# Token-major products with reordered passes, batched norms, earlier operands and masks first in a two-layer decoder kernel

## The chip, the core and the metric

The kernel runs on one core of one Trainium2 chip. The metric is the device time of one execution in microseconds (us). Three runs of the kernel before took 1764.95, 1764.04 and 1764.25 us; the median is 1764.25.

## The reference

The program is a decoder trunk of two layers over 512 tokens of 1024 channels, all in float32. Cut to what matters here, each layer computes

```python
x = x + 0.5 * swiglu(rms_norm(x, ffn1_norm[l]), ffn1_w_in[l], ffn1_w_out[l])   # 1024 -> 2*2816 -> 1024
h = rms_norm(x, mix_norm[l]) @ w_mix_in[l]
(c_x, c_b, c_c, h_q, h_f, h_i, h_g, f_q, f_k, f_v, f_f) = jnp.split(h, split_at, axis=-1)
y = jnp.concatenate([short_conv_mixer(c_x, c_b, c_c, conv_w[l]),               # 256 columns
                     hgrn2_mixer(h_q, h_f, h_i, h_g, lower_bounds[l], ...),    # 4 heads of 64
                     fox_mixer(f_q, f_k, f_v, f_f, ...)], axis=-1)             # 8 heads of 64
x = x + y @ w_mix_out[l]
x = x + 0.5 * swiglu(rms_norm(x, ffn2_norm[l]), ffn2_w_in[l], ffn2_w_out[l])

# fox_mixer, one head, one block of 128 query tokens:
qh = rms_norm(q, q_gain) * 64 ** -0.5;  kh = rms_norm(k, k_gain);  cum = cumsum(log_sigmoid(f + f_bias))
s = qh @ kh.T + (cum[t] - cum[s]);  s = where(t >= s, s, -1e30);  o = softmax(s) @ v
```

## The kernel before

**Precision.** TensorE multiplies in the reduced format `fp32r`. Each float32 operand is therefore split into a high half (a cast on ScalarE, L435) and a low half (the rest, a subtraction on VectorE, L438), and every product is made of three passes into one PSUM bank: high by high (L451), the second pass with a low half (L457), and the third with the other low half (L458). Where the weights move through TensorE and the tokens are stationary, L457 is the pass with the weights' low half `lo`; where the tokens move, L457 and L458 are the two others in the same way. The split weights of two or three rows of tiles are one `hl` tile; there are three such buffers, and two `st` buffers for the loaded weights.

**Stages.** Layer 0's first feed-forward runs from 0 to 341 us of the span, its mixer's projections with HGRN2 to 462, its attention with the output product to 563. Then come the second feed-forward of layer 0 and the first of layer 1, to 1212, layer 1's projections to 1332, its attention to 1432, and its second feed-forward. The change touches the mixer stages of both layers.

**Projections.** Four products are "token-major" (`tokens`): four banks, three named `mm` and one `po`, hold the 128 x 512 results of the four blocks of 128 tokens, and the weights of 512 columns move through. One step of `stream_steps` (a granule) takes two rows of weight tiles: 2 rows x 4 banks x 3 passes = 24 matmuls, handed out in two halves of 12. HGRN2's small matmuls (L1494, 64 of them in a score group, whose bank VectorE empties with the masked copies of L1514) stand between the halves. `fox_qkv` makes two such products for the queries and keys of heads 0-3 and 4-7, and one for the values. ScalarE copies a finished bank into a `qk` tile (L1661). A list `later` holds the root-mean-square norms of the four blocks of a `qk` tile; one entry is issued per half granule (L1644-1655: square, sum, eight small operations on 128 x 8 numbers, and the scaling of 512 columns).

**Attention.** For each head, `prep` transposes a `qk` tile (four transposes, L1697), makes high and low halves (`b`, L1700 on ScalarE, L1701 on VectorE) and copies them with six transfers on the SP queue (L1708) into the stacked operands of the score matmuls. There are 16 steps (h, p), two for each head. `scores` (L1735) fills the score banks: for p = 0 one bank of 128 and 256 columns, for p = 1 two banks of 384 and 512. Each gets two fp32r matmuls and the causal mask, a bf16 matmul of the identity `identb` with `maskb`. VectorE takes the maximum (L1749), ScalarE the exponential and the scaling (L1755, L1757). `turn` transposes the weights `P` two steps later (L1772) and splits them into `PH` and `PL` (L1777, L1778); `values` (L1790) multiplies them with `V` into the `po` bank. At the end of a head, L1803 copies the lower half of the bank, L1804 adds it to the upper one in `fo`; after every second head `fyh` (L1807) and `fyl` (L1808) are the two halves of the 128 rows that go into the output product.

**Output product.** Beside the attention steps runs `most`: for each pair of 128 output channels, two banks take six rows of the mixer's outputs (convolution, HGRN2 and the first heads), three rows at a time, `w_mix_out` stationary and the outputs moving. The last two rows follow behind attention, with `late` passes (L535).

**What sets the order.** One generator per stage hands out dense work; the tables `HGRN_BESIDE` and `BESIDE` say how many half granules stand between two small steps. Where `follow` is called, the instructions of an engine are chained in the order in which they are written ("p" TensorE, "v" VectorE, "a" ScalarE, "s" SyncE); a scheduler places the others.

The loop that sets the order of an attention step is this one:

```python
for k, (h, p) in enumerate(steps):
    turn(h, p)
    if k + 2 < len(steps):
        scores(*steps[k + 2])
    if k:
        values(*steps[k - 1])
    if p == 0 and h + 2 < NH:
        prep(h + 2)
    yield
```

## Time and profile before

| what | us |
|---|---|
| median of three runs | 1764.25 |
| the profiled execution itself | 1765.45 |
| its span | 1763.3 |
| layer 0: projections and HGRN2 (341 to 462) | 121 |
| layer 0: attention and output product (462 to 563) | 101 |
| layer 1: the same two (1212 to 1332, 1332 to 1432) | 120, 100 |
| all else, the feed-forwards | 1321 |

The profile shows one execution. The rows speak of engines: PE is TensorE's matmuls, PEld its loads of stationary operands, DVE VectorE, ACT ScalarE, POOL GpSimd, SP SyncE. A row of the timeline gives the start in us, the duration, the engine, the line of the kernel, the operation and the tiles (out<-in), and in brackets an idle time before it with the instruction that ended it. Matmuls are pipelined: the duration of one is longer than the distance from its start to the next one's, so a loss is read from the starts.

### The profile page before, as it was taken

What the parts mean: (1) busy time and instruction counts of PE and PEld (TensorE: products, weight loads), DVE (VectorE), ACT (ScalarE), POOL (GpSimd) and SP (SyncE); (2) the same over time, 40 slices, a digit from 0 to 9 for tenths busy, and PEclk for the clock granted to TensorE, in tenths of its full rate; (3) what the DMA queues carried; (4) which work ended last, traced back from release to release, by engine and by line L of the source; (5) the groups of instructions that cost most, each with busy time, mean ns of one, the idle gap of its engine ahead of it and who ended that gap; (6) DMA issues with size and microseconds to landing.
All of it is one profiled execution on the core that took longest, in us unless ns stands there. A gap on an engine that the chain in (4) does not pass through costs nothing.

```text
span 1763.3 us, 33430 instructions
## 1 busy us (share of the span) xinstructions
PE 1753.8 (99%) x13613; PEld 1643.2 (93%) x13613; DVE 1416.0 (80%) x1956; ACT 1015.8 (58%) x1433; POOL 177.0 (10%) x174
## 2 busy tenths in 40 slices
PE   9999999999999999999999999999999999999999
PEld 7999999888888899999989999998888889999998
DVE  7988788679777898888679787876888779888783
ACT  5465555466666565555446656555657655655652
POOL 0011120100000111112001111201000001120200
PEclk9999999999999999999999999999999999999999
DMA  7768784243543776869267787923435438687762
GB/s 202 188 140 199 180 177 111 73 124 82 132 118 99 216 163 161 202 169 178 81 183 170 178 182 176 192 79 79 120 93 134 123 103 220 156 176 195 162 138 96
DMA packets 257465, 262.34 MB, mean 149 GB/s; under 512 B 25832, under 2 KB 236528, under 8 KB 257312
## 3 DMA queue, kind: packets, MB, share of 16 engines
q1 hardware_dynamic: 201456, 192.02, 36.4%
q0 software_dynamic: 55840, 68.19, 24.0%
q8 instruction: 107, 1.75, 0.4%
q14 instruction: 46, 0.38, 0.1%
q10 hardware_dynamic: 16, 0.00, 0.0%
HBM read 226.15 MB, written 2.17 MB: 129 GB/s over the span
## 4 chain that ended last, share of the span: by engine, by line
PE 90%; DVE 6%; ACT 2%; issue 1%; DMA 1%; SPq 0%; ACTq 0%; DVEq 0%
PE mm L451 12%; PE mm L458 12%; PE mm L457 12%; PE sc L458 6%; PE sc L451 6%; PE sc L457 6%; PE pt L457 6%; PE pt L451 6%; PE pt L458 6%; PE po L451 3%; PE po L458 3%; PE po L457 3%; DVE hl L438 1%; PE sc L1735 1%; PE po L1790 1%; PE pt L1772 1%
## 5 line engine op out<-in xcount | busy, mean ns | idle before, releaser
L916 DVE TENSOR_TENSOR hl<-w,hl 128x1024 fp32r<-128x1024 f32 x279 | 341.0, 1223 | 91.0 <-ACT hl L914 89.5
L914 ACT CAST hl<-w 128x1024 fp32r<-128x1024 f32 x279 | 292.6, 1049 | 198.3 <-PE mm L458 56.0
L438 DVE TENSOR_TENSOR hl<-st,hl 128x1024 fp32r<-128x1024 f32 (+3 forms) x152 | 160.4, 1056 | 103.0 <-ACT hl L435 101.4
L435 ACT CAST hl<-st 128x1024 fp32r<-128x1024 f32 (+3 forms) x151 | 137.4, 910 | 160.9 <-PE po L458 61.7
L451 PE MATMUL mm<-xc,hl 128*128 128x256 f32 x698 | 191.6, 275 | 0.6 <-ACT u L1034 0.6
L458 PE MATMUL mm<-xc,hl 128*128 128x256 f32 x696 | 191.6, 275 | 0.0
L457 PE MATMUL mm<-xc,hl 128*128 128x256 f32 x696 | 191.5, 275 | 0.0
L451 PE MATMUL pt<-xc,hl 128*128 128x256 f32 x546 | 149.7, 275 | 0.0
L457 PE MATMUL pt<-xc,hl 128*128 128x256 f32 x544 | 149.7, 275 | 0.0
L458 PE MATMUL pt<-xc,hl 128*128 128x256 f32 x544 | 149.6, 275 | 0.0
L451 PEld LDWEIGHTS mm<-xc,hl 128*128 128x128 f32 x698 | 133.9, 192 | 0.9 <-ACT u L1034 0.8
L458 PEld LDWEIGHTS mm<-xc,hl 128*128 128x128 f32 x696 | 133.6, 192 | 0.4 <-DVE hl L916 0.4
L457 PEld LDWEIGHTS mm<-xc,hl 128*128 128x128 f32 x696 | 133.6, 192 | 0.0
L458 PE MATMUL sc<-xc,hl 128*128 128x256 f32 x464 | 127.8, 275 | 0.1
L451 PE MATMUL sc<-xc,hl 128*128 128x256 f32 (+1 forms) x466 | 127.8, 275 | 0.0
L457 PE MATMUL sc<-xc,hl 128*128 128x256 f32 x464 | 127.7, 275 | 0.0
L451 PE MATMUL mm<-x,hl 128*128 128x512 f32 x272 | 105.9, 390 | 0.0
L451 PEld LDWEIGHTS pt<-xc,hl 128*128 128x128 f32 x546 | 104.7, 192 | 0.0
L457 PEld LDWEIGHTS pt<-xc,hl 128*128 128x128 f32 x544 | 104.4, 192 | 0.0
L458 PEld LDWEIGHTS pt<-xc,hl 128*128 128x128 f32 x544 | 104.4, 192 | 0.0
L457 PE MATMUL mm<-x,hl 128*128 128x512 f32 x272 | 103.1, 379 | 0.0
L458 PE MATMUL mm<-x,hl 128*128 128x512 f32 x272 | 103.1, 379 | 0.0
(520 smaller groups left out, 5595.9 us busy)
## 6 DMA issues: line engine op xcount, KB each, us to landing
w<-in_ffn_w_in_dram SPq DMA_DIRECT2D x124, 512.0 KB, 6.0
w<-in_ffn_w_out_dram POOLq DMA_DIRECT2D x50, 512.0 KB, 9.6
w<-in_ffn_w_out_dram SPq DMA_DIRECT2D x49, 512.0 KB, 4.5
st<-in_ffn_w_out_dram SPq DMA_DIRECT2D x39, 512.0 KB, 3.8
st<-in_w_mix_in_dram SPq DMA_DIRECT2D x72, 256.0 KB, 3.0
st<-in_ffn_w_in_dram SPq DMA_DIRECT2D x70, 256.0 KB, 3.5
w<-in_ffn_w_in_dram POOLq DMA_DIRECT2D x29, 512.0 KB, 10.1
w<-S POOLq DMA_DIRECT2D x29, 512.0 KB, 5.1
```

The source lines that it names most:

```text
L435: a = nc.scalar.copy(hi, src[:, c : c + w])
L438: b = nc.vector.tensor_sub(lo, src[:, c : c + w], hi)
L451: i = nc.tensor.matmul(acc[:, c], ah, bh[:, c.start // 2 : c.stop // 2, :], start=first and c.start == 0, stop=False, skip_group_check=True,)
L457: nc.tensor.matmul(acc, ah, bl, start=False, stop=False, skip_group_check=True)
L458: i = nc.tensor.matmul(acc, al, bh, start=False, stop=last, skip_group_check=True)
L914: A(nc.scalar.copy(hi, src))
L916: return lambda: V(nc.vector.tensor_sub(lo, src, hi))
L1735: mm = lambda *a, **k: E(nc.tensor.matmul(*a, skip_group_check=True, **k))
L1772: E(nc.tensor.transpose(tb[:, k * P : (k + 1) * P], to[u][:, j * P : (j + 1) * P], self.ident))
L1790: E(nc.tensor.matmul(self.ob[:, o], half[2][:, j, h].rearrange("p a d -> p (a d)"), part[:, at[0] : at[-1] + 1, :].rearrange("p b t -> p ( ...
```

## The change

The pieces are these.

1. `stream_steps` gets an argument `lows`. In the token-major products (`lows="held"`) the matmuls of each half granule are issued as all high-by-high and tokens-low passes first, and then all passes with the weights' low half. In the output product (`lows="moved"`) the first granule row keeps the three passes together; in the rows after it all passes with the high half of the outputs come first, and those with the low half last. Number and size of the matmuls stay.
2. The norms of the four blocks of a `qk` tile share their small operations: squares and sums go block by block, and then one operation on 128 x 32 numbers stands for four on 128 x 8. The list `later` gets six entries in place of four. VectorE's instructions fall by 58 in all, and ScalarE's by 36.
3. In a score group the mask is the first matmul of its bank, with `start=True`; the two masks of a p = 1 group stand side by side.
4. `prep(h + 2)` stands between `turn` and `scores`, where it stood behind `values`.
5. For the last head VectorE writes the lower rows of the high half `yh` straight from the bank; ScalarE casts only the first 64 rows, which are there earlier.

```diff
--- before.py
+++ after.py
@@ -465,7 +465,7 @@
     def stream_steps(
         self, jobs, parts_of, act, nk, mid=None, pre=None, deal=None, keep=False, lead=False,
-        fine=False, deep=2, rowwise=False, late=False,
+        fine=False, deep=2, rowwise=False, late=False, lows=None,
     ):
@@ -517,6 +517,30 @@
                 if end and not rowwise or lead and k == 0
                 else [(job, j) for j in range(kk) for job in jobs]
             )
+            if lows is not None:
+                if lows == "held":
+                    spans = [order[: len(order) // 2], order[len(order) // 2 :]]
+                    todo = [(x, i) for o in spans for ii in ((0, 2), (1,)) for x in o for i in ii]
+                else:
+                    n0 = len(jobs)
+                    todo = [(x, i) for x in order[:n0] for i in range(3)]
+                    todo += [(x, i) for ii in ((0, 2), (1,)) for x in order[n0:] for i in ii]
+                seen = set()
+                for n, (((acc, cols, toks, *more), j), i) in enumerate(todo):
+                    if n == len(todo) // 2:
+                        yield
+                    x = act(k + j)[i == (1 if lows == "moved" else 2)]
+                    w = rows[j][i == (2 if lows == "moved" else 1)][:, cols]
+                    last = end and all(y is not acc for (y, *_), _ in (t[0] for t in todo[n + 1 :]))
+                    self.follow("p", self.nc.tensor.matmul(
+                        acc, *((w, woven(x)) if toks is None else (x[:, toks], woven(w))),
+                        start=k == 0 and id(acc) not in seen, stop=last, skip_group_check=True,
+                    ))
+                    seen.add(id(acc))
+                k += kk
+                yield
+                continue
             for n, ((acc, cols, toks, *more), j) in enumerate(order):
                 if pre is not None and n == len(order) // 2:
                     pre(k, True)
@@ -1178,7 +1202,7 @@
                 bs = [self.bank(t) for t in ("mm", "mm", "mm", "po")]
                 yield from self.stream_steps(
                     [(bk, slice(0, T), t) for bk, t in zip(bs, TOK)], cols(*spans),
-                    self.xact, KD, lead=True, fine=True, **kw
+                    self.xact, KD, lead=True, fine=True, lows="held", **kw
                 )
                 return bs
@@ -1291,7 +1315,7 @@
                         for n, _ in enumerate(self.stream_steps(
                             [(bk, c, None) for bk, c in zip(banks, FM2)],
                             rows(0, 256 * dg, 256), act(0), 6, keep=True, fine=True, deep=3,
-                            rowwise=True,
+                            rowwise=True, lows="moved",
                         )):
                             if dg == 0 and n == 1:
                                 self.conv_out(ap_, 1, last)
@@ -1635,24 +1659,35 @@
                     later.pop(0)()
                 yield
-        def norm(qk, i):
-            x = qk[:, i].rearrange("p h w d -> p (h w) d")
-            sq = hp.tile([P, 8, HD], F32, tag="fs", name=self.n("fs"))
-            s8 = lambda tag: mp.tile([P, 8], F32, tag=tag, name=self.n(tag), bufs=2)
-            m, r, t = s8("fm"), s8("fr"), s8("ft")
-            nc.scalar.activation(sq, x, AF.Square)
-            nc.vector.reduce_sum(m, sq, axis=AX.X)
-            nc.vector.tensor_scalar(
-                m, m, scalar1=self.inv2[:, i : i + 1], scalar2=None, op0=ALU.mult
-            )
-            self.act(r, m, AF.Ln, bias=self.epsc)
-            self.act(r, r, AF.Exp, scale=-0.5)
-            self.rsqrt(r, m, r, t)
-            nc.vector.tensor_scalar(
-                r, r, scalar1=self.invc[:, i : i + 1], scalar2=None, op0=ALU.mult
-            )
-            nc.vector.tensor_mul(x, x, r.unsqueeze(2).to_broadcast([P, 8, HD]))
+        def norms(qk):
+            small = lambda tag: mp.tile([P, 4, 8], F32, tag=tag, name=self.n(tag), bufs=2)
+            m, r, t = small("fm"), small("fr"), small("ft")
+            wide = lambda a: a.unsqueeze(2).to_broadcast([P, 4, 8])
+            def squares(i):
+                x = qk[:, i].rearrange("p h w d -> p (h w) d")
+                sq = hp.tile([P, 8, HD], F32, tag="fs", name=self.n("fs"))
+                nc.scalar.activation(sq, x, AF.Square)
+                nc.vector.reduce_sum(m[:, i], sq, axis=AX.X)
+            def finish():
+                nc.vector.tensor_mul(m, m, wide(self.inv2))
+                self.act(r, m, AF.Ln, bias=self.epsc)
+                self.act(r, r, AF.Exp, scale=-0.5)
+                self.rsqrt(r, m, r, t)
+                nc.vector.tensor_mul(r, r, wide(self.invc))
+            def scale(i):
+                x = qk[:, i].rearrange("p h w d -> p (h w) d")
+                nc.vector.tensor_mul(x, x, r[:, i].unsqueeze(2).to_broadcast([P, 8, HD]))
+            later.append(lambda: squares(0))
+            later.append(lambda: squares(1))
+            later.append(lambda: squares(2))
+            later.append(lambda: (squares(3), finish()))
+            later.append(lambda: (scale(0), scale(1)))
+            later.append(lambda: (scale(2), scale(3)))
         for hf in range(2):
             qk = mp.tile([P, 4, 4, 2, HD], F32, tag="qk", name=self.n("qk"), bufs=2)
@@ -1662,7 +1697,7 @@
                     qk[:, i].rearrange("p h w d -> p w h d"),
                     bank.rearrange("p (h d w) -> p w h d", w=2, h=4),
                 )
-                later.append(lambda qk=qk, i=i: norm(qk, i))
+            norms(qk)
             half.append(qk)
         V = mp.tile([P, 4, NH, 2, HD], F32R, tag="V", name=self.n("V"))
         half.append(V)
@@ -1729,20 +1764,19 @@
                 at = [b[:, :P], b[:, P : 3 * P]]
             else:
                 at = [self.bank("sc")[:, : 3 * P], self.bank("sc")]
+            mm = lambda *a, **k: E(nc.tensor.matmul(*a, skip_group_check=True, **k))
+            if p == 0:
+                masked = [b.rearrange("p (b t) -> p b t", t=P)[:, ::2, :]]
+            else:
+                masked = [at[u][:, (2 + u) * P : (3 + u) * P] for u in range(2)]
+            for m in masked:
+                mask = self.maskb.unsqueeze(1).to_broadcast([P, 2, P]) if p == 0 else self.maskb
+                mm(m, self.identb, mask, start=True, stop=False)
             for u in range(2):
                 i = 2 * p + u
                 c, n = slice(i * P, (i + 1) * P), (i + 1) * P
-                mm = lambda *a, **k: E(nc.tensor.matmul(*a, skip_group_check=True, **k))
-                mm(at[u], QA[:, c], KA[:, :n], start=p == 1 or u == 0, stop=False)
-                mm(at[u], QB[:, c], KB[:, :n], start=False, stop=False)
-                if p == 1:
-                    mm(at[u][:, c], self.identb, self.maskb, start=False, stop=True)
-                elif u == 1:
-                    mm(
-                        b.rearrange("p (b t) -> p b t", t=P)[:, ::2, :], self.identb,
-                        self.maskb.unsqueeze(1).to_broadcast([P, 2, P]), start=False, stop=True,
-                    )
+                mm(at[u], QA[:, c], KA[:, :n], start=False, stop=False)
+                mm(at[u], QB[:, c], KB[:, :n], start=False, stop=True)
             to = [pb[:, :P], pb[:, P:]] if p == 0 else [pb[:, : 3 * P], pb[:, 3 * P :]]
             for u in range(2):
                 o = slice(u, u + 1)
@@ -1801,10 +1835,16 @@
             fo = self.fo
             ft = tl(self.tt, self.tb)
             nc.scalar.copy(ft[r, :], self.ob[64:, :])
+            if h == NH - 1:
+                kt = 4 + h // 2
+                nc.scalar.copy(self.yh[kt][:64, :], fo[:64, :])
+                nc.vector.tensor_add(self.yh[kt][r, :], self.ob[:64, :], ft[r, :])
             nc.vector.tensor_add(fo[r, :], self.ob[:64, :], ft[r, :])
             if h % 2:
                 kt = 4 + h // 2
-                nc.scalar.copy(self.yh[kt], fo)
+                if h < NH - 1:
+                    nc.scalar.copy(self.yh[kt], fo)
                 nc.vector.tensor_sub(self.yl[kt], fo, self.yh[kt])
         steps = [(h, p) for h in range(NH) for p in range(2)]
@@ -1817,12 +1857,12 @@
         yield
         for k, (h, p) in enumerate(steps):
             turn(h, p)
+            if p == 0 and h + 2 < NH:
+                prep(h + 2)
             if k + 2 < len(steps):
                 scores(*steps[k + 2])
             if k:
                 values(*steps[k - 1])
-            if p == 0 and h + 2 < NH:
-                prep(h + 2)
             yield
         values(*steps[-1])
```

TensorE in layer 0's attention, at a step in which `prep` stands. The tiles are `pt` for the transposes' banks, `sc` for the score bank, S and q for the operands of the scores. Before:

```order
L1772 MATMUL pt_5326<-ident,P_5197 128x128 x3
L1735 MATMUL sc_5335<-S_655_5216,S_654_5215 128x128
L1735 MATMUL sc_5335<-q_657_5218,q_656_5217 128x128
L1735 MATMUL sc_5335<-S_655_5216,S_654_5215 128x256
L1735 MATMUL sc_5335<-q_657_5218,q_656_5217 128x256
L1735 LDWEIGHTS identb
L1735 MATMUL sc_5335<-maskb,identb 128x2x128
L1697 MATMUL pt_5355<-ident,qk_4158 128x128 x4
```

TensorE at the same place in the changed kernel:

```order
L1806 MATMUL pt_5260<-ident,P_5131 128x128 x3
L1732 MATMUL pt_5273<-ident,qk_4158 128x128 x4
L1767 LDWEIGHTS identb
L1767 MATMUL sc_5289<-maskb,identb 128x2x128
L1767 MATMUL sc_5289<-S_637_5150,S_636_5149 128x128
L1767 MATMUL sc_5289<-q_639_5152,q_638_5151 128x128
L1767 MATMUL sc_5289<-S_637_5150,S_636_5149 128x256
L1767 MATMUL sc_5289<-q_639_5152,q_638_5151 128x256
```

The four transposes of `prep` and the mask moved from behind the score matmuls to the place ahead of them.

TensorE in the output product, the end of the second granule of the first pair of output channels, just ahead of the transposes of `P` (`cyh` is the high half of a convolution output, `fyh` and `fyl` are halves of the first heads' output). Before:

```order
L458 MATMUL mm_5848<-cyh_3684,hl_5941 128x512
L451 MATMUL mm_5847<-fyh_636_5142,hl_5941 128x512
L457 MATMUL mm_5847<-fyl_640_5146,hl_5941 128x512
L458 MATMUL mm_5847<-fyh_636_5142,hl_5941 128x512
L1772 MATMUL pt_5955<-ident,P_5818 128x128 x4
```

TensorE there in the changed kernel:

```order
L536 MATMUL mm_5782<-cyh_3684,hl_5875 128x512
L536 MATMUL mm_5781<-fyh_618_5072,hl_5875 128x512 x2
L536 MATMUL mm_5782<-fyh_618_5072,hl_5875 128x512
L1806 MATMUL pt_5889<-ident,P_5752 128x128 x4
L1806 MATMUL pt_5896<-ident,P_5752 128x128 x3
```

The pass with `fyl` left this half granule for the end of the next one, and a pass with `fyh` took its place.

VectorE in layer 0's projections, around the masked copies that empty HGRN2's score banks (`fr` is the norm's factor, `qk` the tile that it scales). Before:

```order
L438 TENSOR_TENSOR hl_4855<-st_4853,hl_4855 128x1024
L1652 TENSOR_SCALAR fr_4634<-fr_4634,invc_3901 128x8
L1514 COPY_PREDICATED A_4325<-lmask,sc_4647 128x64x2
L1655 TENSOR_TENSOR qk_4158<-qk_4158,fr_4634 128x512
L1514 COPY_PREDICATED A_4325<-lmask,sc_4648 128x64x2
L1471 TENSOR_TENSOR t_4685<-t_4689,q_3707 128x256
L1514 COPY_PREDICATED A_4325<-lmask,sc_4647 128x32x4
L1514 COPY_PREDICATED A_4325<-lmask,sc_4648 128x32x4
```

VectorE there in the changed kernel:

```order
L1683 TENSOR_TENSOR qk_4158<-qk_4158,fr_4474 128x512 x3
L438 TENSOR_TENSOR hl_4825<-st_4823,hl_4825 128x1024
L1538 COPY_PREDICATED A_4325<-lmask,sc_4610 128x64x2
L1538 COPY_PREDICATED A_4325<-lmask,sc_4611 128x64x2
L1538 COPY_PREDICATED A_4325<-lmask,sc_4610 128x32x4
L1538 COPY_PREDICATED A_4325<-lmask,sc_4611 128x32x4
```

The scalings of `qk` stand ahead of the weights' low half, and the four masked copies stand together behind it.

## The prediction

> **What bounds the kernel now.** I read the page first, then the busy time by stage, then the rows of TensorE in order of time wherever the distance from one matmul's start to the next is longer than the matmul's columns explain, and last the rows of the engine that each such gap names. Three lines of the page and two of the stages, layer 0's projections with HGRN2 and layer 0's attention with the output product (columns: stretch and its length; busy time of PE, PEld, DVE, ACT, POOL; granted clock; DMA share; GB/s):
>
> ```profile
> span 1763.3 us, 33430 instructions
> PE 1753.8 (99%) x13613; PEld 1643.2 (93%) x13613; DVE 1416.0 (80%) x1956; ACT 1015.8 (58%) x1433; POOL 177.0 (10%) x174
> PE 90%; DVE 6%; ACT 2%; issue 1%; DMA 1%; SPq 0%; ACTq 0%; DVEq 0%
> 341.00:462.00 121.00, 120.18 (x1113) 102.35 (x1113) 95.90 (x225) 74.87 (x147) 6.17 (x11) 1.00 0.43 108
> 462.00:563.00 101.00, 99.62 (x578) 86.13 (x577) 73.62 (x141) 65.44 (x141) 3.10 (x6) 1.00 0.44 117
> ```
>
> TensorE is busy 99% and carries 90% of the chain, at a granted clock of 1.00. No matmul of 512 or 256 columns is removed or added, so the time can fall only by gaps between matmuls, and rise only by new ones. The change touches the two mixer stages alone. So the work is to price each gap there, and to ask what each moved instruction will now keep waiting.
>
> **Token products: the pass with the weights' low half goes last.** The first granule of the first token product in layer 0:
>
> ```profile
> 376.23 0.38 PE L451 MATMUL mm<-hl,x 128*128 128x512 f32 x1
> 377.20 0.48 PE L457 MATMUL mm<-hl,x 128*128 128x512 f32 x1 [0.59 <-DVE hl L438]
> 377.52 0.38 PE L458 MATMUL mm<-hl,x 128*128 128x512 f32 x1
> 375.93 1.22 DVE L438 TENSOR_TENSOR hl<-st,hl 128x1024 fp32r<-128x1024 f32 x1
> ```
>
> L457 multiplies the low half `lo`, which VectorE finishes at 377.15. From L451 to L458 it is 1.29 us, two matmuls; two that wait for nothing take 0.43 (one, 516.64 to 516.86 in a fence below, is 0.22). That is 0.86 us, in layer 0 only. In the new order eight matmuls with `hi` come ahead, 1.7 us at 0.216, and the low half is needed at about 378.0: the gap closes, and the cover is 0.8 us. In all other granules the low half comes in time and the new order is worth nothing. The number of stationary loads stays: each matmul has one now and then.
>
> What is late next: the fourth bank of a piece was wanted by the next piece after 18 matmuls, now after 16, 0.43 us sooner.
>
> ```profile
> 407.10 0.57 ACT L1661 COPY qk<-po 128x512 f32<-128x512 f32 x1
> 408.07 0.38 PE L451 MATMUL po<-hl,x 128*128 128x512 f32 x1
> ```
>
> The copy that empties the bank ends at 407.67, the bank is wanted at 408.07: 0.40 us of room against 0.43. I charge 0.03 for each layer, -0.06. The bounds are 0 (the small norm step that stood ahead on ScalarE is gone) and 0.43 each, -0.86. The bank that finishes later itself (10th of 24 matmuls for the 6th) still has 14 matmuls, 3.0 us, to a copy of 0.57.
>
> **Norms: small steps at once.** 60 instructions leave VectorE and 36 ScalarE, each of 8 columns; one of 32 columns now does the work of four. Neither engine is the bound, so this is worth what it moves out of the way of TensorE. One place shows it, in both layers:
>
> ```profile
> 421.15 0.73 DVE L1655 TENSOR_TENSOR qk<-qk,fr 128x512 f32<-128x512 f32 x1
> 422.39 0.47 DVE L1514 COPY_PREDICATED A<-lmask,sc 128x128 f32<-128x128 uint8 x2
> 422.25 0.38 PE L458 MATMUL po<-hl,x 128*128 128x512 f32 x1
> 422.82 0.27 PE L1494 MATMUL sc<-t,t 64*64 64x32 f32 x2 [0.19 <-DVE A L1514]
> 1293.28 0.21 PE L1494 MATMUL sc<-t,t 64*64 64x32 f32 x1 [0.19 <-DVE A L1514]
> ```
>
> HGRN2's next score group starts 0.57 us after a matmul that needs 0.22; it waits for the masked copies that empty its bank. Between their halves VectorE scales a `qk` tile for 0.73 us. In the new order all four scalings stand ahead of that granule's low half and nothing but the copies behind it, so they end some 0.6 us sooner: 0.35 x 2 = 0.70 us. The bounds are 0 and 0.70; that the three scalings in a row delay the low half ahead of the copies is covered by the pass order above (1.7 us).
>
> **Operands sooner.** `prep(h+2)` goes from behind the scores and values of a step to the place ahead of them, with its four transposes, ScalarE's and VectorE's halves and six copies on the SP queue.
>
> ```profile
> 480.12 0.69 ACT L1700 ACTIVATE b<-pt,qkg 128x512 fp32r<-128x512 f32 x1
> 482.69 1.85 SPq L1708 DMA_DIRECT2D q<-b  x1
> 486.20 0.49 PE L1772 MATMUL pt<-ident,P 128*128 128x128 f32 x3
> 487.03 0.30 PE L1735 MATMUL sc<-S,S 128*128 128x128 f32 x1 [0.34 <-DMA S<-b]
> 488.11 0.28 PE L1735 MATMUL sc<-maskb,identb 128*128 128x256 bf16 x1
> 1356.61 0.49 PE L1772 MATMUL pt<-ident,P 128*128 128x128 f32 x3
> 1357.41 0.28 PE L1735 MATMUL sc<-maskb,identb 128*128 128x256 bf16 x1
> ```
>
> From the transposes to the mask it is 1.91 us in layer 0 and 0.80 in layer 1: the scores of head 3 wait 1.11 us for the operand copies, after one SP issue of 1.85 us. In the new order the ScalarE half starts about 2 us sooner and four transposes and the mask (0.44 + 0.12) stand between. So the wait goes where it exists. Whether unprofiled runs have it I can't see; the profiled execution took 1765.45, 1.20 over the median. I take half, 0.55; bounds 0 and 1.11. On the SP queue three loads for the output product fall behind these copies (about 4 us); they are cast 14 us after their issue, so nothing waits.
>
> **Output product: the low half of the tokens last.**
>
> ```profile
> 515.76 0.62 ACT L1807 CAST fyh<-fo 128x512 fp32r<-128x512 f32 x1
> 516.64 0.38 PE L458 MATMUL mm<-cyh,hl 128*128 128x512 f32 x1
> 516.86 0.38 PE L451 MATMUL mm<-fyh,hl 128*128 128x512 f32 x1
> 517.68 0.48 PE L457 MATMUL mm<-fyl,hl 128*128 128x512 f32 x1 [0.45 <-DVE fyl L1808]
> 1386.98 0.48 PE L457 MATMUL mm<-fyl,hl 128*128 128x512 f32 x1 [0.45 <-DVE fyl L1808]
> ```
>
> The start is 0.82 us after the last where 0.22 would do, and the matmul itself is 0.10 longer after the wait (0.48 for 0.38): 0.70 a layer, 1.40. Now only `fyh` matmuls stand in this half granule, and `fyh` is there at 516.38; `fyl` is wanted a whole attention step later. Bounds 1.2 and 1.4.
>
> **The last head's high half straight from the bank.**
>
> ```profile
> 559.59 0.68 DVE L1804 TENSOR_TENSOR fo<-po,t 64x512 f32<-64x512 f32 x1
> 560.30 0.62 ACT L1807 CAST fyh<-fo 128x512 fp32r<-128x512 f32 x1 [1.40 <-DVE fo L1804]
> 560.35 0.38 PE L458 MATMUL pt<-fyh,hl 128*128 128x512 f32 x1
> 560.98 0.70 PE L535 MATMUL sc<-fyh,hl 128*128 128x512 f32 x2 [0.24 <-ACT fyh L1807]
> ```
>
> TensorE stands for 0.63 - 0.22 = 0.41 us a layer. VectorE now writes `fyh` itself by 560.27 and the cast of 0.62 leaves the chain, so the 0.41 go whole: 0.82. The added addition of 0.68 puts `fyl` at about 561.7, and eight matmuls (1.7 us) come ahead of its use.
>
> **Masks first.** A score group of the second kind, and what follows:
>
> ```profile
> 543.20 0.42 PE L1735 MATMUL sc<-S,S 128*128 128x384 f32 x1
> 543.64 0.23 PE L1735 MATMUL sc<-maskb,identb 128*128 128x128 bf16 x1
> 543.68 0.48 PE L1735 MATMUL sc<-S,S 128*128 128x512 f32 x1
> 544.00 0.40 PE L1735 MATMUL sc<-q,q 66*128 66x512 f32 x1
> 544.24 0.23 PE L1735 MATMUL sc<-maskb,identb 128*128 128x128 bf16 x1
> 544.28 0.37 PE L1790 MATMUL po<-PH,V 128*128 128x256 f32 x1
> ```
>
> After a bf16 mask the next matmul starts at once (0.04) but holds the engine for 0.32 instead of 0.22: with 0.04 against the 0.056 of 128 columns, 0.085 a change of kind. Two masks side by side make one such change for two, in 8 groups of 2 layers: 16 x 0.085 = 1.36 us. How a mask behind fp32 transposes behaves no row shows. If it costs the dearest change seen, 0.10, in all 32 groups, the term is 1.36 - 3.2 = -1.84; if the groups of the first kind lose theirs too, 32 x 0.085 = 2.72. I take 1.36, since the transposes' own change to fp32r stood there before. The Trainium skill (TensorE: Matmul & The Clock Gate, sections LDWEIGHTS and Weight-path perf modes) gives a stationary load as columns over 1.2 GHz, and a faster one for 128 weights that aren't fp32. As an estimate by that page, a mask of 53 ns covers half of the next load of 107 ns, so one such rest of 53 ns would go in each of 16 groups, 0.85 us, and the sum would be 0.5 smaller.
>
> **The sum.** 0.86 + 0.70 + 0.55 + 1.40 + 0.82 + 1.36 - 0.06 = 5.63 us. Against the profiled execution's own 1765.45 that is 1759.8; its 1.20 over the median are in no term but the halved one, so I set the sum against the median of 1764.25: 1758.6.
>
> **Rivals.** *Masks behind transposes cost a change of kind.* For it: every change from transposes or masks to fp32r shows about 0.1. Against it: the identity is short. The sum becomes 2.4: 1761.8.
>
> *The vector and scalar chain sets the pace of the projections.* For it: the bank above has 0.40 us of room. Then TensorE's 0.86 and 0.70 return as waits a little later, and the wait for the copies was of that one execution: 3.5 remain, 1760.7. Against it: in layer 1 the same stage passes with neither the 0.86 nor a later wait.
>
> *ScalarE's order turns against attention: slower.* Its cast of P and the operand half (0.47 + 0.69) now come ahead of the scaling of the next weights.
>
> ```profile
> 477.55 1.22 ACT L1755 ACTIVATE P<-P,rs 128x384 f32<-128x384 f32 x2
> 481.30 0.49 PE L1772 MATMUL pt<-ident,P 128*128 128x128 f32 x3
> ```
>
> The scaling ends at 478.77, its transposes start at 481.30: 2.5 us of room for the 1.16. If ScalarE also stands for those transposes, more than 2.5 is used and each of 12 operand steps can lose up to 1.16: 14 us, 1773 or less. It decides from 0.76 a step (5.6 + 3.5 over 12). The Trainium skill (TensorE: Matmul & The Clock Gate, table at its head) calls ScalarE's queue a strict FIFO, which is this rival's premise; the 1.40 us that ScalarE stood at 560.30 agrees.
>
> **Chances and range.** The forecast 0.60, masks 0.13, vector chain 0.14, ScalarE 0.13. A measurement of this kernel tells about 0.2%, 3.5 us, from no change: below 1760.7 is faster, above 1767.8 slower. Faster: 0.56 of the forecast's 0.60 and a third of the vector rival's 0.14, 0.61; slower: most of the ScalarE rival, 0.11; same 0.28. The forecast's own range is 1756.2 (copies whole, masks at their better bound, 0.5 for what I don't see) to 1760.7; with the two rivals on its side and 1.7 for bank waits beyond my bound it reaches to 1763.5.
>
> **What would show it.** Right: no wait for `hl` L438 at the first token product, none for the masked copies near 422, none for `fyl` or `fyh`; layer 0's attention stage in some 99 us. The masks: distance from the last transposes to the first fp32r matmul of a group. Wrong: idle TensorE in front of `pt` transposes of P, named ScalarE; or a wait for a `qk` copy at the start of the second token product.

## The result, and the profile after

The changed kernel takes 1760.83 us (median of 17 runs, 1760.01 to 1762.14); the kernel before took 1764.25 in its 17 runs beside them. The ratio is 0.998, with a 95% interval of 0.9974 to 0.9987: faster by 3.4 us, in an interval of 2.3 to 4.6. The forecast was 1758.6, 5.6 us faster, in a range of 1756.2 to 1763.5. So the time lies in the range, but a tenth above 1760.7, where the forecast's own part of it ends; beyond that it had been widened for the rivals. Some 2 us of the expected gain did not come.

The page of the changed kernel, its first line and the busy time:

```profile
span 1758.5 us, 33346 instructions
PE 1749.8 (100%) x13613; PEld 1644.2 (93%) x13613; DVE 1410.7 (80%) x1898; ACT 1009.7 (57%) x1397; POOL 177.2 (10%) x174
```

To see the mixers apart from the feed-forwards, the starts of two rows are subtracted in each layer: from the first matmul with `ones_mean` ahead of the projections to the last matmul with `fyh`. In layer 0 of the kernel before these are the two rows here, from the timeline:

```profile
341.26 1.02 PE L609 MATMUL pt<-sqa,ones_mean 128*128 128x512 f32 x2
568.63 0.38 PE L458 MATMUL po<-fyh,hl 128*128 128x512 f32 x1
```

In the changed kernel the same two matmuls start at 340.34 and 564.99. That is 227.37 us before and 224.65 after. Layer 1 went from 225.19 to 224.08. Both layers together, here called **the mixers**, went from 452.56 to 448.73, by 3.83. Cut further at the first transpose of `qk` and the last matmul of values:

| stretch | before | after | gain |
|---|---|---|---|
| layer 0, projections | 105.65 | 104.78 | 0.87 |
| layer 0, attention | 110.90 | 109.56 | 1.34 |
| layer 0, end | 10.82 | 10.31 | 0.51 |
| layer 1, projections | 104.58 | 104.14 | 0.44 |
| layer 1, attention | 109.79 | 109.64 | 0.15 |
| layer 1, end | 10.82 | 10.31 | 0.51 |

Layer 1's attention stands out: masks, the wait for `fyl` and nothing else were to save 1.4 us there, and it saved 0.15.

The rows that answer to those of before come from the timeline of the changed kernel. **The first token product** of layer 0:

```profile
375.31 2.75 PE L536 MATMUL mm<-hl,x 128*128 128x512 f32 x12
378.43 1.13 PE L536 MATMUL mm<-hl,x 128*128 128x512 f32 x4 [0.37 <-DVE zf L1253]
377.01 1.22 DVE L438 TENSOR_TENSOR hl<-st,hl 128x1024 fp32r<-128x1024 f32 x1
378.15 0.22 DVE L1253 SCALAR_TENSOR_TENSOR zf<-mm,invc,fb 128x8 f32<-128x8 f32 x1
```

The first twelve matmuls run without the wait for the low half. But the thirteenth opens the third `mm` bank, and VectorE reads that bank for `zf` only at 378.15, behind another low half of 1.22 us. The wait is new at this place. From 377.69, the start of the twelfth (eleven steps of 0.216 from 375.31), to 378.43 it is 0.74, of which 0.53 is lost. The matmul behind it is 0.10 longer: four take 1.13 us, where four without a wait take 1.03 (three steps of 0.216 and one of 0.38).

**HGRN2's score group and the masked copies:**

```profile
419.63 1.06 DVE L1538 COPY_PREDICATED A<-lmask,sc 128x128 f32<-128x128 uint8 x4
420.86 0.38 PE L536 MATMUL po<-hl,x 128*128 128x512 f32 x1
421.17 0.55 PE L1518 MATMUL sc<-t,t 64*64 64x32 f32 x23
```

The four copies stand in one piece and end at 420.69; the score group starts 0.31 us after the last matmul, as it does at all other groups.

**Attention in layer 0**, the scores of head 3:

```profile
484.37 0.49 PE L1806 MATMUL pt<-ident,P 128*128 128x128 f32 x3
485.13 0.27 PE L1767 MATMUL sc<-maskb,identb 128*128 128x256 bf16 x1
485.16 0.31 PE L1767 MATMUL sc<-S,S 128*128 128x128 f32 x1
485.31 0.28 PE L1767 MATMUL sc<-q,q 66*128 66x128 f32 x1
```

Head 3 no longer waits for its operand copies. Now head 2 in layer 1, with its semaphore instructions (from the view by source line):

```profile
1343.52 0.30 PE L1767 MATMUL sc<-A 128*128 128x128 f32 x1
1343.84 0.30 PE L1767 MATMUL sc<-kb,kb 66*128 66x128 f32 x1
```

```profile
L1767 PEldq EVENT_SEMAPHORE  x4: 51/51/51, 1343.3 to 1343.7; - x4
```

Here the second score matmul starts 0.32 us after the first, where head 3 takes 0.15 (485.16 to 485.31). Four separate semaphore instructions of 51 ns stand there between mask and scores. From the transposes to the next dense matmul (one of 512 columns) this step takes 0.32 us more than the like steps of other heads in layer 1, and 0.22 more in layer 0.

**The output product**, in the order of time:

```profile
516.34 0.62 ACT L1376 CAST cyh<-cu 128x512 fp32r<-128x512 f32 x1 [0.65 <-DVE cu L1374]
516.66 0.43 PE L536 MATMUL mm<-fyh,hl 128*128 128x512 f32 x1
517.01 1.13 PE L536 MATMUL mm<-cyh,hl 128*128 128x512 f32 x4
518.07 1.14 DVE L1783 TENSOR_REDUCE nm<-sc 128x1 f32<-128x384 f32 x2
518.85 0.81 PE L536 MATMUL mm<-hy,hl 128*128 128x512 f32 x3
519.13 0.68 DVE L1309 TENSOR_TENSOR xT<-mm,xT 128x512 f32<-128x512 f32 x1
519.87 0.92 PE L536 MATMUL mm<-hy,hl 128*128 128x512 f32 x3 [0.21 <-DVE xT L1309]
531.60 2.29 PE L536 MATMUL mm<-hy,hl 128*128 128x512 f32 x9
```

The wait for `fyl` is gone in both layers. Others stand in its place. The second convolution output `cyh` is ready at 516.96 and is now wanted at 516.88, since its high passes moved ahead of the low ones. It starts 0.35 after `fyh`; the kernel with late operands below shows 0.27 there without a wait, so 0.08 is lost. And the next pair of channels wants its second bank after three matmuls, at 519.50; VectorE adds that bank into `xT` only from 519.13, behind two maxima that take 1.14 us together (0.37 lost). Each is followed by a matmul that is 0.10 longer. Layer 1 has the same two. A third, small one stands at the pair after that: the nine matmuls from 531.60 take 2.29 us, where nine without a stop take 2.11, so 0.18 is lost (0.08 and 0.10), in layer 1 too. That is 0.18, 0.47 and 0.18: 0.83 a layer.

**The last head:**

```profile
556.43 0.69 DVE L1842 TENSOR_TENSOR fyh<-po,t 64x512 fp32r<-64x512 f32 x1
557.22 0.38 PE L458 MATMUL pt<-fyh,hl 128*128 128x512 f32 x1
557.43 0.59 PE L559 MATMUL sc<-fyh,hl 128*128 128x512 f32 x2
```

The start of L559 follows by 0.21: no wait.

### The profile page after: what moved, and what is told of

Read it like the earlier page. It is cut to its first block, busy times and chain, and to the rows that moved or that the text cites. A ratio compares the mean times of both kernels' runs of the same rounds, so it can differ in the third digit from the quotient of the medians.

```text
span 1758.5 us, 33346 instructions
## 1 busy us (share of the span) xinstructions
PE 1749.8 (100%) x13613; PEld 1644.2 (93%) x13613; DVE 1410.7 (80%) x1898; ACT 1009.7 (57%) x1397; POOL 177.2 (10%) x174
## 4 chain that ended last, share of the span: by engine, by line
PE 92%; DVE 5%; ACT 1%; issue 1%; DMA 1%; SPq 0%; ACTq 0%; DVEq 0%
PE mm L451 10%; PE mm L458 10%; PE mm L457 10%; PE mm L536 8%; PE sc L458 6%; PE sc L451 6%; PE sc L457 6%; PE pt L457 6%; PE pt L451 6%; PE pt L458 6%; PE po L451 3%; PE po L457 3%; PE po L458 3%; PE po L536 2%; PE sc L1767 1%; DVE hl L438 1%
## 5 line engine op out<-in xcount | busy, mean ns | idle before, releaser
L451 PE MATMUL mm<-xc,hl 128*128 128x256 f32 x698 | 191.6, 275 | 0.1
L457 PE MATMUL mm<-xc,hl 128*128 128x256 f32 x696 | 191.5, 275 | 0.0
L451 PE MATMUL pt<-xc,hl 128*128 128x256 f32 x546 | 149.7, 275 | 0.0
L457 PE MATMUL pt<-xc,hl 128*128 128x256 f32 x544 | 149.7, 275 | 0.0
L451 PEld LDWEIGHTS mm<-xc,hl 128*128 128x128 f32 x698 | 133.9, 192 | 0.3 <-ACT u L1058 0.3
L457 PEld LDWEIGHTS mm<-xc,hl 128*128 128x128 f32 x696 | 133.6, 192 | 0.0
L451 PE MATMUL sc<-xc,hl 128*128 128x256 f32 (+1 forms) x466 | 127.7, 275 | 0.0
L457 PE MATMUL sc<-xc,hl 128*128 128x256 f32 x464 | 127.7, 275 | 0.0
L536 PE MATMUL mm<-hl,x 128*128 128x512 f32 x432 | 108.3, 386 | 0.4 <-DVE zf L1253 0.4
L451 PE MATMUL mm<-x,hl 128*128 128x512 f32 x272 | 105.4, 388 | 0.0
L451 PEld LDWEIGHTS pt<-xc,hl 128*128 128x128 f32 x546 | 104.7, 192 | 0.0
L457 PEld LDWEIGHTS pt<-xc,hl 128*128 128x128 f32 x544 | 104.4, 192 | 0.0
L458 PE MATMUL mm<-x,hl 128*128 128x512 f32 x272 | 103.1, 379 | 0.0
```

Of the source, the lines that this page charges most:

```text
L451: i = nc.tensor.matmul(acc[:, c], ah, bh[:, c.start // 2 : c.stop // 2, :], start=first and c.start == 0, stop=False, skip_group_check=True,)
L457: nc.tensor.matmul(acc, ah, bl, start=False, stop=False, skip_group_check=True)
L458: i = nc.tensor.matmul(acc, al, bh, start=False, stop=last, skip_group_check=True)
L536: self.follow("p", self.nc.tensor.matmul(acc, *((w, woven(x)) if toks is None else (x[:, toks], woven(w))), start=k == 0 and id(acc) not i ...
```

## The experiments

All runs were compared with the kernel before on the same chip; its medians beside them were 1764.55 us (first four experiments below), 1764.59 (next four) and 1764.26 (last four). The medians of single kernels are uncertain by some tenths, so the mixers' time from the profiled execution stands beside them: it leaves out the feed-forwards, which no experiment touches. It is the time of one execution, and waits vary: the one for `zf` loses 0.49 to 0.78 in the seven traces that have it, so a difference of 0.3 or less in the mixers says little unless rows carry it. The kernel before was profiled in an execution 1.20 over its median; the gains of the mixers against it may be some tenths too large. The rows shown below are from the timeline of the kernel that the section is on; the starts and what stands in brackets carry the reading.

| kernel | median us | ratio to before, 95% interval | mixers us |
|---|---|---|---|
| before | 1764.25 | | 452.56 |
| the change | 1760.83 | 0.9974 to 0.9987 | 448.73 |
| change, old output order | 1760.87 | 0.9972 to 0.9990 | 448.95 |
| change, masks last | 1761.49 | 0.9974 to 0.9992 | 449.07 |
| change, operands late | 1760.57 | 0.9970 to 0.9987 | 448.24 |
| change, old token order | 1760.39 | 0.9968 to 0.9987 | 448.63 |
| change, old norms | 1762.36 | 0.9978 to 0.9996 | 450.26 |
| change, old last head | 1761.82 | 0.9976 to 0.9994 | 449.86 |
| change, one row moved | 1760.17 | 0.9967 to 0.9985 | 448.25 |
| change, other bank | 1759.81 | 0.9965 to 0.9985 | 448.17 |
| before, masks first alone | 1762.86 | 0.9984 to 1.0002 | 450.74 |
| before, batched norms alone | 1762.77 | 0.9983 to 1.0001 | 450.76 |
| change, bank and lead | 1759.25 | 0.9963 to 0.9981 | 446.90 |
| change, bank, lead, head 3 alone early | 1757.81 | 0.9952 to 0.9977 | 445.89 |

### Output product in the old order

```diff
-                            rowwise=True, lows="moved",
+                            rowwise=True,
```

> The changed kernel with the output product's passes in the old order, all else as changed. Theory A (what the two traces of before and after show): the wait for fyl closed, worth 0.7 us a layer, but in its place the new order waits for the second convolution output (0.24) and, at the start of the next pair of channels, for the addition that empties the bank (0.47), so it is worth about 0: this kernel takes the same as the changed one, 1760.8 within 0.5; the row with the wait for fyl is back in both layers and the two new waits are gone. Rival B (the prediction's own term): the order is worth 1.40 us and the missing gain was lost elsewhere: 1762.2.

Measured: 1760.87, the mixers 0.22 longer. The timeline's row:

```profile
514.22 0.38 PE L451 MATMUL mm<-fyh,hl 128*128 128x512 f32 x1
515.29 0.48 PE L457 MATMUL mm<-fyl,hl 128*128 128x512 f32 x1 [0.69 <-DVE fyl L1848]
```

The wait for `fyl` is back, and longer than in the kernel before: 1.07 us from start to start, for 0.82. The new waits are gone. Of the 0.22, 0.11 stand in the two attention stretches, where the order was changed, so the new order is worth some 0.1 to 0.2 us within the change, and not 1.40. Theory A holds.

### Masks last

```diff
-            for m in masked:
-                mask = self.maskb.unsqueeze(1).to_broadcast([P, 2, P]) if p == 0 else self.maskb
-                mm(m, self.identb, mask, start=True, stop=False)
...
+                if p == 1:
+                    mm(at[u][:, c], self.identb, self.maskb, start=False, stop=True)
```

> The changed kernel with the masks behind the scores as before. Theory A: only the groups of the second kind gain by masks first, 0.07 us in each of 16, 1.1 us; groups of the first kind are equal: 1761.9. In the trace, second-kind groups return from 0.64 to about 0.71 us above the time of their columns. Rival B: a mask behind transposes costs a change of kind and the masks are worth nothing or less: 1760.8 or below. In the step of head 2 the score matmuls also wait for semaphores behind the mask (0.22 and 0.32 us); if the mask's place causes that, it goes here.

Measured: 1761.49, the mixers 0.34 longer. Taken from the transposes of `P` to the next dense matmul, less the time of the columns, a score group of the second kind takes 0.71 us (0.64 with masks first) and the first kind 0.69 (0.68). The step of head 2 is at 0.69 too (0.90 and 1.00 with masks first): the semaphores cost nothing there when the scores stand ahead of the mask. Group by group the masks gain what theory A says, about 1.0 us in 14 groups, and the semaphores take back 0.54; the rest, 0.46, is what the two attention stretches show (0.26 and 0.20), and the mixers as a whole 0.34.

### Operands late

```diff
-            if p == 0 and h + 2 < NH:
-                prep(h + 2)
             if k + 2 < len(steps):
                 scores(*steps[k + 2])
             if k:
                 values(*steps[k - 1])
+            if p == 0 and h + 2 < NH:
+                prep(h + 2)
```

> The changed kernel with the operands of head h+2 made behind scores and values as before. Theory A: the wait of 1.11 us for the operand copies of head 3 in layer 0 comes back, and the two new waits at head 2 (0.22 and 0.32 us) go, since the semaphores are then passed earlier: 0.6 slower than the changed kernel, 1761.4. Rival B: the wait of 1.11 was of one execution; then the earlier operands are worth 0 or cost 0.5: 1760.3 to 1760.8, and the trace shows no gap ahead of the scores of head 3.

Measured: 1760.57, the mixers 0.49 *shorter*. Both theories missed something. Head 3 of layer 0 does wait again; the second fence is the convolution output:

```profile
485.41 0.30 PE L1767 MATMUL sc<-S,S 128*128 128x128 f32 x1
485.98 0.30 PE L1767 MATMUL sc<-q,q 66*128 66x128 f32 x1 [0.27 <-DMA q<-b]
```

```profile
517.73 0.43 PE L536 MATMUL mm<-fyh,hl 128*128 128x512 f32 x1
518.00 1.03 PE L536 MATMUL mm<-cyh,hl 128*128 128x512 f32 x4
```

That step is 0.61 us longer than in the change. But the semaphores' cost at head 2 is gone, and so is the wait for the second convolution output, which neither theory had put down to the operands: from `fyh` at 517.73 to `cyh` at 518.00 it is 0.27, where the change takes 0.35. In layer 1, where head 3 never waited, the attention is 0.57 us shorter; in layer 0 it is 0.21 longer. So early operands gain 0.6 at one place and lose some 1.0 at others. All four traces with late operands (before, this one and the two parts alone below) have the wait of head 3: against the same step of layer 1 it takes 1.11, 0.66, 1.13 and 0.95 us.

### Token products in the old order

```diff
-                    self.xact, KD, lead=True, fine=True, lows="held", **kw
+                    self.xact, KD, lead=True, fine=True, **kw
```

> The changed kernel with the token-major products' passes in the old order. Theory A: the wait for the weights' low half (0.86 us) comes back in layer 0 and the new wait for the bank that VectorE's zf still reads (0.6 us) goes: 0.3 slower than the changed kernel, 1761.1. Rival B: the order is worth the predicted 0.86 less 0.06: 1761.6, and the wait for zf stands in this kernel too.

Measured: 1760.39, the mixers 0.10 shorter. The rows:

```profile
376.18 0.38 PE L451 MATMUL mm<-hl,x 128*128 128x512 f32 x1
376.99 0.48 PE L457 MATMUL mm<-hl,x 128*128 128x512 f32 x1 [0.43 <-DVE hl L438]
```

The wait for the low half is back (0.81 us from L451 to L457, for 0.22), the one for `zf` is gone. The new order of the token products is worth nothing here that one execution could show.

### The norms block by block

```diff
-            norms(qk)
+                later.append(lambda qk=qk, i=i: norm(qk, i))
```

> The changed kernel with the norms block by block as before. Theory A: the waits for the masked copies come back (0.35 us in front of HGRN2's score group, both layers) with the small pauses inside that group (0.15): the two projection stages become 0.4 to 0.5 us longer each, 0.9 us in all, 1761.7. Rival B: VectorE's 58 instructions were also what let the rest of the change stand, and more waits come back than these (the one for zf in layer 0 grows): 1.5 us or more, above 1762.3.

Measured: 1762.36, the mixers 1.53 longer: 0.90 and 0.74 more in the projections, a little less in the attention. The wait for the masked copies is back, and larger than it was in the kernel before:

```profile
423.05 0.38 PE L536 MATMUL po<-hl,x 128*128 128x512 f32 x1
423.84 0.88 PE L1518 MATMUL sc<-t,t 64*64 64x32 f32 x33 [0.41 <-DVE A L1538]
```

0.79 us stand between the starts, 0.57 before. The size is rival B's (1.5), but the wait for `zf` did not grow as B had it (0.58 lost for 0.53): it is the wait for the masked copies that does. The change has only the norms and the new order of the passes in the projections, so the order of the passes is what is left to have raised it.

### The last head's cast as before

```diff
-                nc.vector.tensor_add(self.yh[kt][r, :], self.ob[:64, :], ft[r, :])
...
+                nc.scalar.copy(self.yh[kt], fo)
```

> The changed kernel with the last head's fyh cast by ScalarE from fo as before. Theory A: the wait of 0.41 us with the 0.10 behind it returns at the end of attention in both layers, 1.02 us in all and nothing else: 1761.85, the stretch from the last value matmul to the last fyh matmul goes from 10.31 to 10.82 us. Rival B: the added addition on VectorE costs part of it elsewhere, and the undone version is less than 0.5 slower: below 1761.3.

Measured: 1761.82. The stretch at the end takes 10.80 us in both layers, for 10.31: 0.98 in all.

```profile
557.52 0.38 PE L458 MATMUL pt<-fyh,hl 128*128 128x512 f32 x1
558.12 0.48 PE L559 MATMUL sc<-fyh,hl 128*128 128x512 f32 x1 [0.23 <-ACT fyh L1841]
```

Theory A holds in place and size.

### One row moved

```diff
-                    todo += [(x, i) for ii in ((0, 2), (1,)) for x in order[n0:] for i in ii]
+                    todo += [(x, i) for ii in ((0, 2), (1,)) for x in order[n0 : 2 * n0] for i in ii]
+                    todo += [(x, i) for x in order[2 * n0 :] for i in range(3)]
```

> The changed kernel with one row of each output-product granule, the second, in the new order (high passes, then the low half) and the third with its three passes together again. Theory A: the new waits are due to the third row alone: the one for the second convolution output (0.14 and 0.10 behind it) and the one at the next pair of channels for the addition that empties the bank (0.37 and 0.10) go, the one for fyl stays away: 0.7 us a layer, 1.4 in all, 1759.4. Rival B: VectorE's queue sets these times, and a wait for fyl or for the addition stands there again: 1760.8.

Measured: 1760.17, the mixers 0.48 shorter, not 1.4.

```profile
517.20 0.38 PE L537 MATMUL mm<-cyh,hl 128*128 128x512 f32 x1
517.58 0.48 PE L537 MATMUL mm<-cyl,hl 128*128 128x512 f32 x1
518.76 1.43 PE L537 MATMUL mm<-hy,hl 128*128 128x512 f32 x4
518.97 1.28 DVE L1310 TENSOR_TENSOR xT<-mm,xT 128x512 f32<-128x512 f32 x2
```

`cyh` is in time, but its low half `cyl` is not (0.16), and the addition still begins at 518.97, so the second bank of the next pair waits for it still: the four `hy` matmuls take 1.43 us, where four without a wait take 1.03. The start that is late loses 0.29, for 0.37 in the change. VectorE's queue is what is late in this stretch, and whichever pass comes first meets it: the waits are rival B's, and the size lies between the two forecasts.

### Another bank

```diff
-                bv = [self.bank(t) for t in ("mm", "sc", "sc", "po")]
+                bv = [self.bank(t) for t in ("pt", "sc", "sc", "po")]
```

> The changed kernel with the first of the four banks of the product ahead of the token products taken from the transposes' banks in place of the third token bank. Theory A: the wait of 0.53 us (and 0.10 behind) at the first token product of layer 0 is for zf, which reads that bank late on VectorE; with another bank it goes and nothing takes its place: 0.6 us, 1760.2. Rival B: VectorE and ScalarE set the pace there, and the next granule's weights or the fourth bank (po, read by zf last) are waited for: 1760.8.

Measured: 1759.81, the mixers 0.56 shorter. Sixteen matmuls now run without a stop where twelve did:

```profile
374.77 3.62 PE L536 MATMUL mm<-hl,x 128*128 128x512 f32 x16
378.41 0.92 PE L536 MATMUL po<-hl,x 128*128 128x512 f32 x3
```

The fourth bank, read by the last `zf`, costs 0.18 at 378.41, which theory A did not expect. Layer 0's projections, where the wait stood, are 0.39 shorter; the rest of the 0.56 lies where nothing was changed. The cause of the new wait in the token product is the bank, as theory A has it.

### Masks first alone

The kernel before, with the loop over `masked` of the change and nothing else.

> The kernel before with masks first alone. Theory A: taken back from the changed kernel the masks were worth 0.34 us in the mixer stages, because the earlier operands had put them where four semaphore instructions stand between mask and scores at head 2; alone they are worth the full 0.07 in each of 16 groups of the second kind, 1.1 us: 1763.4 against 1764.5 before. Rival B: the masks themselves bring the semaphores into the open, and 0.3 to 0.5 is all: 1764.1.

Measured: 1762.86 (the interval reaches just over 1). The attention stretches are 0.69 and 0.70 us shorter, 1.39 in all. Groups of the second kind take 0.63, before 0.72. Head 2's step takes 0.66, so the semaphores cost nothing without the early operands. The remaining 0.4 of the mixers' gain lies in layer 0's projections and is the wait for the first low half, 0.39 us in this execution and 0.75 in that of before. Theory A, by a little more than expected.

### Batched norms alone

The kernel before, with `norms` of the change and nothing else.

> The kernel before with the batched norms alone. Theory A: 1.53 us of the mixer stages came back when the norms were undone in the changed kernel, because the new pass order had raised the wait for the masked copies from 0.35 to 0.58; alone they are worth the smaller wait, 0.35 and the 0.10 behind it with the 0.15 inside the group, 1.0 us for both layers: 1763.5. Rival B: the norms themselves are worth the 1.53: 1763.0; or, as predicted, 0.70: 1763.8.

Measured: 1762.77 (the interval reaches just over 1 here too). In layer 1 the projections take 104.06 us for 104.58, 0.52; in layer 0 the gain is 0.82, of which 0.21 is again the varying wait for the low half. The wait for the masked copies is gone:

```profile
420.35 0.38 PE L458 MATMUL po<-hl,x 128*128 128x512 f32 x1
420.66 0.95 PE L1494 MATMUL sc<-t,t 64*64 64x32 f32 x51
```

That makes 0.5 to 0.6 a layer, 1.1: theory A by these rows. The mixers as a whole are 1.80 shorter; 0.45 of that is in the attention, where nothing was changed (0.2 of it the wait of head 3), so neither the mixers nor the median tells theory A from rival B here. The 1.53 of the undone norms holds a price that the norms alone don't show, and that came with the new pass order.

### Bank and lead

```diff
-                            rowwise=True, lows="moved",
+                            rowwise=True, lows="moved", lead=dg > 0,
...
-                bv = [self.bank(t) for t in ("mm", "sc", "sc", "po")]
+                bv = [self.bank(t) for t in ("pt", "sc", "sc", "po")]
```

> The changed kernel with the other bank for the product ahead of the token products, and with the first granule of the output product's second to fourth pair of channels finishing its first bank ahead of its second. Theory A: the wait for the addition that empties the second bank (0.37 and 0.10 a layer) goes, since that bank is wanted 1.1 us later, and with the 0.56 of the bank the mixer stages go from 448.73 to 447.2: 1759.3. Rival B: VectorE sets the pace of that stretch, the wait stands somewhere behind: 1760.2.

Measured: 1759.25, the mixers at 446.90. The first granule of the next pair of channels begins so:

```profile
520.08 1.46 PE L536 MATMUL mm<-hy,hl 128*128 128x512 f32 x6
```

Six `hy` matmuls in 1.46 us is the time without a stop. Theory A, by a little more than expected, since the small wait at the third pair is gone too: a bank that is wanted after eight matmuls in place of three hides the late addition. The attention stretches are 0.65 and 0.74 shorter than in the change.

### Bank, lead, and early operands for head 3 alone

```diff
+            if p == 0 and h == 1:
+                prep(3)
             if k + 2 < len(steps):
                 scores(*steps[k + 2])
             if k:
                 values(*steps[k - 1])
-            if p == 0 and h + 2 < NH:
+            if p == 0 and h + 2 < NH and h != 1:
                 prep(h + 2)
```

> As the one before, and the operands are made early for head 3 alone, late for all others. Theory A: the semaphores at head 2 (0.22 and 0.32 us) and the wait for the second convolution output (0.24 a layer) were the price of the early operands of the other heads; they go, and the wait of head 3 in layer 0 stays away: 1.0 less, 1758.3. Rival B: moving operands changes nothing here, 1759.3, or head 3 waits again, 1759.0.

Measured: 1757.81 in five runs (1757.35 to 1757.99), 1.4 us below the version without this step and below every one of the changed kernel's 17. The mixers take 445.89, 1.01 less.

```profile
515.96 0.43 PE L536 MATMUL mm<-fyh,hl 128*128 128x512 f32 x1
516.23 1.03 PE L536 MATMUL mm<-cyh,hl 128*128 128x512 f32 x4
517.96 1.46 PE L536 MATMUL mm<-hy,hl 128*128 128x512 f32 x6
```

No wait for `cyh`, none for the addition, none at head 2 or head 3. Theory A. This version beats both kernels: 6.4 us under the one before.

Head 2 deserves a second look, because the operands of head 3 are made early here, so that TensorE has the same order at head 2's scores as in the change: transposes of `P`, transposes of `qk`, mask, scores. The rows of the change first, then those of this version:

```profile
473.88 1.14 DVE L1783 TENSOR_REDUCE nm<-sc 128x1 f32<-128x384 f32 x2
474.48 0.49 PE L1806 MATMUL pt<-ident,P 128*128 128x128 f32 x3
```

```profile
472.72 1.14 DVE L1783 TENSOR_REDUCE nm<-sc 128x1 f32<-128x384 f32 x2
474.03 0.49 PE L1806 MATMUL pt<-ident,P 128*128 128x128 f32 x3
474.36 0.60 PE L1732 MATMUL pt<-ident,qk 128*128 128x128 f32 x4
474.82 0.31 PE L1767 MATMUL sc<-A 128*128 128x128 f32 x1
474.97 0.28 PE L1767 MATMUL sc<-kb,kb 66*128 66x128 f32 x1
```

The second score matmul follows the first by 0.23 in the change (475.39 to 475.62) and by 0.15 here. The four semaphore instructions run from 475.2 to 475.5 in the change, around the mask, and from 474.1 to 474.4 here, among the transposes. VectorE's two maxima end 0.54 us behind the start of the transposes in the change, and 0.17 ahead of it here.

## Why the prediction was right in sign and too large

The terms, with what undoing each part in the changed kernel cost in the mixers:

| term | predicted | undone in the change | what the runs show |
|---|---|---|---|
| token products | 0.86 | -0.10 | the wait went, another of 0.53 and 0.10 came |
| bank of the next product | -0.06 | | no wait for a `qk` copy shows |
| norms | 0.70 | 1.53 | 1.1 alone |
| operands | 0.55 | -0.49 | 0.6 gained at head 3 (1.1 against before), 1.0 lost elsewhere |
| output product | 1.40 | 0.22 | the wait went, three of 0.83 a layer in all came |
| last head | 0.82 | 1.13 | 0.98 at the place |
| masks | 1.36 | 0.34 | 1.39 alone |

The undone parts sum to 2.63, the change to 3.83: the parts lean on one another, and the table is no sum. A balance can be drawn from the rows instead. What went: 0.85 at the first low half, 1.1 by the norms, 1.11 at head 3, 1.42 at `fyl`, 1.02 at the last head and 1.39 by the masks, 6.9 us. What came: 0.63 at `zf`, 1.66 in the output product and 0.54 at head 2, 2.8. That leaves 4.1, where the mixers show 3.83.

So two errors met. The stalls that the change removes were worth more than forecast (6.9 for 5.7), and the new waits, for which the sum held 0.06, cost 2.8. That the time still fell into the range is in part luck: the first error paid for some of the second.

**The step that failed** is "the gap closes, and the cover is 0.8 us" in the token products, and the like step in the output product, "`fyl` is wanted a whole attention step later". Both are true of the operand that they speak of. What they left out is what else TensorE wants sooner once it no longer stops: the third bank, which `zf` still holds, and `cyh` and the second bank of the next pairs. "What is late next" was asked for one bank only, the `po` bank of the next piece, and that one was in time. Of the 0.86 us 0.63 came back, and of the 1.40 all: the rows of the new waits add up to 1.66, and taking the order back costs 0.1 to 0.2.

**Operands.** "So the wait goes where it exists" held, and halving it was too careful: all four traces with late operands have it. The price was looked for on the SP queue alone, where "nothing waits"; what the move does to VectorE's and TensorE's own order stood in no term. That undoing the move brings `cyh` back in time, and head 2 back to its usual length, is shown. The move is not the whole of it: with the operands early and the masks last, `cyh` starts 0.27 behind `fyh` too, and only the 0.09 behind it is left. Which VectorE instruction pushed them is not traced further.

**Layer 1's attention** now adds up: 0.70 by the masks and 0.71 at `fyl`, less 0.32 at head 2 and 0.83 in the output product, leaves 0.26, and it saved 0.15.

**Masks.** The price of a change of kind was right: 1.36 forecast, 1.39 measured alone. The sentence on the Trainium skill (TensorE: Matmul & The Clock Gate) gave an estimate of 0.85 for the same; the run decides for the row. The rival, that masks behind transposes cost a change of kind in all groups, is out: the first kind is equal to 0.01 us. In the change the semaphores took 0.54 back; the last version, masks first too, doesn't lose them.

**Norms and last head** were undersized. For both, the 0.10 that the matmul behind a wait is longer was left out, though the output product's term had it: 0.51 a layer for 0.41 at the last head. The small pauses inside the score group were left out as well. The norms also hid what the new token order would have cost at the masked copies (0.58 lost where the kernel before lost 0.35).

**The rivals.** "The vector and scalar chain sets the pace of the projections" gave 1760.7, nearest to the measured time, and of its "TensorE's 0.86 and 0.70 return as waits a little later" the 0.86 is what happened. Its 0.70 did not return, and it looked for the chain in the projections alone, while the larger return, 0.83 us a layer, is in the output product; so its nearness in time is luck too. ScalarE's order did not turn against attention: no wait for ScalarE stands in front of the transposes of `P`. The 1.40 us for which ScalarE stood at 560.30 tests nothing of its order: its next cast there waited for TensorE until 563.91.

## What to carry to other kernels

When a reordering removes a stall, list every bank and operand that the waiting engine opens in the next few microseconds, with the time at which its last reader or writer is done, and not only the nearest one; the engine that was late stays late, and the stall moves to the next thing that it serves. Two cheap remedies worked here: take the next bank from another pool, and finish one bank before opening the second. Moving a step earlier for all iterations, when one of them waits, can cost the others more than that one gains.

## What was not expected of the hardware

Four semaphore instructions of 51 ns on TensorE's queue cost 0.22 to 0.32 us at head 2 in the change, and nothing with the masks last, with the operands late, with the masks alone, or in the last version (0.64 to 0.69 us for the step). The first three suggest that it takes the transposes of the operands and the mask directly ahead of the scores; the last version has both and pays nothing, so that is not enough. What goes with the cost in every trace is VectorE's time: in the eight traces that pay, in both layers, its two maxima end 0.52 to 0.55 us behind the start of the transposes of `P` and the semaphore instructions run some 0.7 us behind that start; in the three that have masks first and don't pay, the maxima end 0.15 to 0.17 us ahead of it and the semaphores run from 0.05 us on. The last of head 2's copies is issued 4.3 us ahead of its scores in the change (471.05 to 475.39) and 4.2 in the last version (470.62 to 474.82), so a later landing is unlikely. No run moves VectorE's order alone, so the cause is not shown.

The first matmul after a wait is 0.10 us longer than its neighbours in the cases met here with 512 columns (0.48 for 0.38). A wait isn't needed for it: behind HGRN2's small matmuls of 32 columns, without any stop, four matmuls take 1.13 us too (at 409.35 in the change).
